# The ordering pass works under its timeline simulation of engines and transfers instead of its simpler estimate: a transformer block on one core

## The chip, the core and the metric

One Trainium2 chip, of which the program uses one core. A core has five engines, each with its own queue of instructions: TensorE (PE, matrix products), VectorE (DVE), ScalarE (ACT), GpSimd (POOL) and SyncE (SP, which here only starts transfers). The metric is the device time of one execution in microseconds (us); of several runs the median is taken.

## The reference, cut to what matters

One block over 1024 tokens of width 1024, with 256 context tokens in front of it:

```python
px = split_proj(modulate(layer_norm(x), ...) @ w_in)            # q, k, v of attention; q, k, v, z of the delta rule; two gates
# differential attention, 8 heads: two softmaxes over 1280 keys, subtracted
p = softmax(q @ k.T); a = p[0] - lam * p[1]; o_da = rms_norm(a @ v)
# gated delta rule, 8 heads, forward and backward in time: a recurrence over chunks
for chunk: v_new = u - w @ state; o = q @ state + qk @ v_new; state = state * g + k.T @ v_new
y = (sigmoid(g1) * (o_da @ w_br_da) + sigmoid(g2) * (o_dn @ w_br_dn)) @ w_o
h = layer_norm(alpha * h + gate * y); h = layer_norm(alpha * h + gate * (relu(u @ w1) ** 2 @ w2))
```

All is fp32. A large product is done as three products of split operands (a high and a low part each).

## The kernel before

The code names operations and tiles; a pass of the library then puts all instructions of the program in one order. It goes through the program with a priority for each instruction and an estimate of when engines and transfers are free, gives each engine the ready instruction of the first priority, and writes the order out. Each engine then runs its own instructions in exactly that order, and waits on semaphores where an operand isn't there. So nothing is chosen at run time: what the pass put behind a waiting instruction on the same engine waits too. The code sets the priorities by `rank`: in the stages below a recurrence or a softmax has class 0, its preparation 1, and the projections that fill the gaps come after them.

The stages, in the order of time:

1. Norms, modulation, projections of the context.
2. The delta rule (`dn_phase`), head by head. For head h: `dn_proj` (a projection of `cvraw`, then seven taps of a convolution: one on ACT and six on DVE for each of two parts, L440, into `kT`, `qT`, `vT`), `dn_prep` (decays, L467 and L470; Gram matrices, L520 and L528; a triangular inverse on DVE, `inverse32`), `dn_double` (small products that complete the inverse, L611 to L633), then `dn_chain`: ten steps in each of two directions, each step L676, a DVE operation (L678), L680, ACT (L683, L686), L688, DVE (L693), and the output (L698, L699, and on DVE L706, L707). At its end the output of the head, `oacc`, is normed (L715 to L719) and transposed on PE (L723). `kT` and `qT` have two buffers each, so the taps of head h + 2 wait until the last step of head h has read them.
3. Attention (`da_all`): 64 tiles of 128 queries, eight for each head. `da_scores` of a tile: score products into `sx` (two maps, 1024 keys each) and `sc` (256 context keys), L877 and L878; maxima on DVE (L887 to L889), exponentials on ACT (L893, L894) into `p`, sums and the difference of the maps on DVE (L897 to L903). `da_values` of a tile, one tile later in the code: ten transposes of `p` into one bank `pat` (L913) in groups of 3, 3, 3 and 1, each group copied out into `aT` by ACT, DVE, ACT and ACT (L914), then ten products with `V` (L916), then `oh` (L917, L918). `p` of map 0 has one buffer, of map 1 two; each `sx` has one.
4. Merge of the branches, norms, and the MLP (L974 to L976, L1370).

The fillers are the projections, three products of 128x512 for each of eight blocks of the width and two halves of the tokens (`gemm_cols`, L164 to L166): 48 for one weight. They need nothing of the recurrence or the softmax that runs beside them. Three weights, 144 products, belong to the next head in the attention stage. In the last attention head the products of `branch_dn` (L974 to L976) take their place.

## Time and profile before

| | |
|---|---|
| median of three runs | 3041.43 us (3039.56 to 3043.84) |
| the profiled execution: its time, its span | 3038.64 us, 3036.9 us |
| PE busy | 93% of the span |
| DVE, ACT, POOL busy | 66%, 44%, 22% |
| granted TensorE clock, mean | 0.958 |

The span runs from the first instruction to the last. An engine's busy share is a mean over stages that are limited in different ways. [...]

### The profile page before, as it was taken

To read this page: it belongs to the slowest core of one execution; us is meant where nothing else is said; L and a number is where in the kernel's file an instruction comes from. 1 tells how busy PE (TensorE), PEld (TensorE's weight loads), DVE (VectorE), ACT (ScalarE), POOL (GpSimd) and SP (SyncE) were. 2 spreads that over 40 slices of the span, in tenths; PEclk is the share of its full clock that TensorE was granted. 3 is DMA by queue.
4 is the path that set the end of the run, shared out by engine and by line. 5 is a ranking of instruction groups with operands and counts; after the bars stand their busy time and mean duration, and the time that the engine had idled before them with its cause. 6 is when DMAs were issued, how large, how long until landed. Compare 5 with 4: busy or idle time off the path is not lost. (4 is left out here: it accounts for less than half of the span.)

```text
span 3036.9 us, 44469 instructions
## 1 busy us (share of the span) xinstructions
PE 2828.2 (93%) x15928; PEld 2273.6 (75%) x15928; DVE 2008.3 (66%) x3675; ACT 1333.1 (44%) x3269; POOL 656.6 (22%) x756
## 2 busy tenths in 40 slices
PE   7998989899898999989999999899999999989998
PEld 4886768677686777868887778677777677768887
DVE  4768497794967767247777778664486776544435
ACT  4655244444443544326655556564465422322210
POOL 1234223532423241021111110101001643100000
PEclk9999799998998999789999999999999999999999
DMA  7631211211212122173433332416564544453321
GB/s 253 190 110 43 52 48 34 67 53 41 70 33 66 34 63 67 37 186 81 105 93 93 91 88 66 91 39 198 158 220 131 164 143 120 137 194 104 104 63 63
DMA packets 340973, 303.09 MB, mean 100 GB/s; under 512 B 87892, under 2 KB 287700, under 8 KB 339728
## 3 DMA queue, kind: packets, MB, share of 16 engines
q1 hardware_dynamic: 318864, 252.14, 28.5%
q10 hardware_dynamic: 18304, 37.41, 4.8%
q0 software_dynamic: 3584, 10.71, 1.0%
q8 instruction: 125, 2.05, 0.3%
q14 instruction: 96, 0.79, 0.1%
HBM read 212.08 MB, written 66.06 MB: 92 GB/s over the span
## 5 line engine op out<-in xcount | busy, mean ns | idle before, releaser
L150 POOL TENSOR_TENSOR wlo<-wraw,whi 128x256 fp32r<-128x256 f32 x312 | 320.7, 1033 | 1219.5 <-ACT whi L149 987.3
L164 PE MATMUL pg<-uh,whi 128*128 128x512 f32 x1152 | 481.7, 418 | 6.6 <-ACT whi L149 3.2
L166 PE MATMUL pg<-uh,wlo 128*128 128x512 f32 x1152 | 481.3, 418 | 6.1 <-POOL wlo L150 5.8
L165 PE MATMUL pg<-ul,whi 128*128 128x512 f32 x1152 | 481.4, 418 | 0.0
L149 ACT CAST whi<-wraw 128x256 fp32r<-128x256 f32 (+1 forms) x568 | 241.0, 430 | 322.9 <-PE pg L165 102.9
L166 PEld LDWEIGHTS pg<-uh,wlo 128*128 128x128 f32 x1152 | 224.6, 195 | 49.9 <-POOL wlo L150 11.1
L164 PEld LDWEIGHTS pg<-uh,whi 128*128 128x128 f32 x1152 | 224.9, 195 | 47.0 <-ACT whi L149 4.8
L165 PEld LDWEIGHTS pg<-ul,whi 128*128 128x128 f32 x1152 | 224.8, 195 | 39.6
L1370 PE MATMUL pa<-B,A 128*128 128x512 f32 x768 | 220.6, 395 | 13.6 <-ACT B L1318 5.0
L1370 PE MATMUL pg<-B,A 128*128 128x512 f32 x768 | 219.5, 393 | 0.0
L150 DVE TENSOR_TENSOR wlo<-wraw,whi 128x256 fp32r<-128x256 f32 (+1 forms) x256 | 136.6, 542 | 120.8 <-ACT whi L149 119.1
L888 DVE TENSOR_REDUCE mp<-sx 128x1 f32<-128x1024 f32 x128 | 155.7, 1218 | 49.8 <-PE sx L878 49.4
L1370 PEld LDWEIGHTS pa<-B,A 128*128 128x128 f32 x768 | 145.9, 190 | 46.9 <-ACT B L1318 5.4
L1370 PEld LDWEIGHTS pg<-B,A 128*128 128x128 f32 x768 | 146.2, 190 | 30.7
L893 ACT ACTIVATE p<-sx,mx 128x1024 f32<-128x1024 f32 x128 | 143.2, 1118 | 53.2 <-DVE mx L889 41.9
L916 PEld LDWEIGHTS pat<-V,aT 128*128 128x128 f32 x1280 | 151.0, 193 | 14.6 <-ACT aT L914 12.1
L916 PE MATMUL pat<-V,aT 128*128 128x128 f32 x1280 | 158.8, 279 | 0.0
L913 PE MATMUL pat<-ident,p 128*128 128x128 f32 x640 | 119.6, 285 | 8.0 <-ACT oh L917 5.0
L1386 DVE TENSOR_TENSOR acc<-pa,acc 128x512 f32<-128x512 f32 x32 | 22.1, 690 | 157.0 <-PE pa L1370 157.0
L1318 ACT CAST A<-araw 128x1024 fp32r<-128x1024 f32 x32 | 33.6, 1052 | 209.7 <-PE pg L1370 171.8
L913 PEld LDWEIGHTS pat<-ident,p 128*128 128x128 f32 x640 | 74.6, 142 | 56.2 <-ACT aT L914 21.3
L877 PE MATMUL sx<-K,Q 128*128 128x512 f32 x256 | 109.5, 428 | 2.9 <-DMA wraw<-in_w_in_dram 2.0
(457 smaller groups left out, 6701.8 us busy)
## 6 DMA issues: line engine op xcount, KB each, us to landing
wraw<-in_w_in_dram SPq DMA_DIRECT2D x288, 128.0 KB
wraw<-in_w_in_dram SPq DMA_DIRECT2D x64, 256.0 KB
uraw<-in_w_mlp_dram SPq DMA_DIRECT2D x32, 512.0 KB
braw<-in_w_mlp_dram SPq DMA_DIRECT2D x32, 512.0 KB
araw<-ff_d SPq DMA_DIRECT2D x32, 512.0 KB
ff_d<-ue SPq DMA_DIRECT2D x52, 256.0 KB
adraw<-in_w_ada_dram SPq DMA_DIRECT2D x32, 320.0 KB
wa<-in_w_ada_dram SPq DMA_DIRECT2D x8, 1024.0 KB
```

What stands on the lines that cost most here:

```text
L149: nc.scalar.copy(out=hi, in_=raw)
L150: self.weng.tensor_tensor(out=lo, in0=raw, in1=hi.bitcast(F32), op=ALU.subtract)
L164: nc.tensor.matmul(o, lhsT=hi, rhs=a, start=k == 0, stop=False)
L165: nc.tensor.matmul(o, lhsT=hi, rhs=b, start=False, stop=False)
L166: nc.tensor.matmul(o, lhsT=lo, rhs=a, start=False, stop=k == KT - 1)
L877: nc.tensor.matmul(ps, lhsT=Q[m][:, qs], rhs=Kh[m][:, ks], start=True, stop=False)
L888: nc.vector.tensor_reduce(out=mp[:, m, 0:1], in_=px[m], axis=AX.X, op=ALU.max)
L893: nc.scalar.activation(out=p[:, CTX:], in_=px[m], func=AF.Exp, bias=mx[:, m:m + 1], accum_out=sp[:, 0, m:m + 1])
L913: nc.tensor.transpose(out=pt[:, c], in_=a[:, (c0 + c) * P:(c0 + c + 1) * P], identity=self.ident)
L916: nc.tensor.matmul(po, lhsT=aT[:, c], rhs=r["v"][:, c], start=c == 0, stop=c == NT - 1)
L1318: nc.scalar.copy(out=z[:, 0], in_=x)
L1370: mm = lambda x, y, **kw: nc.tensor.matmul(ps[c], lhsT=a[:, x, k], rhs=bt[:, y, s], **kw)
```

## The change

One argument of the context that records and orders the program. No operation, tile, buffer or priority changes.

```diff
-    with tile.TileContext(nc) as tc:
+    with tile.TileContext(nc, schedule_with_timeline_sim=True) as tc:
```

The pass still goes by the priorities, but what is ready and free comes from a simulation of the engines' queues and of the transfers. Both programs hold the same instructions on PE, DVE, POOL and SP; ACT has six loads of function tables more (nine instead of three at other lines). The order on every engine differs over the first two thirds of the program; the second product of the MLP (L1370) stands as before.

**Place 1: PE and DVE inside an attention head.** On PE `p` and `pat` belong to a tile's values, `sx` to the scores of a later tile, `pg` is a filler's product. Before, the transposes of one tile (`p_17524`) stand between fillers:

```order
L913 MATMUL pat<-ident,p_17524 128x128 x3
L166 MATMUL pg<-uh,wlo 128x512
L164 MATMUL pg<-uh,whi 128x512
L165 MATMUL pg<-ul,whi 128x512
L166 MATMUL pg<-uh,wlo 128x512
L913 MATMUL pat<-ident,p_17524 128x128 x3
L164 MATMUL pg<-uh,whi 128x512
L165 MATMUL pg<-ul,whi 128x512
L166 MATMUL pg<-uh,wlo 128x512
L913 MATMUL pat<-ident,p_17524 128x128
```

Now, in a tile of the same place (`p_16413`; its copies out of `pat` still come after 3, 3, 3 and 1 transposes):

```order
L913 MATMUL pat<-ident,p_16413 128x128 x9
L877 MATMUL sx_16579<-K_16007,Q_16101 128x512
L878 MATMUL sx_16579<-L_16009,Q_16101 128x512
L877 MATMUL sx_16579<-K_16007,Q_16101 128x512
L878 MATMUL sx_16579<-L_16009,Q_16101 128x512
L913 MATMUL pat<-ident,p_16413 128x128
L916 MATMUL pat<-V,aT 128x128 x10
```

The fillers are gone from between the transposes, and half of the scores of the tile three places on (`sx_16579`) now stand ahead of the last transpose. From the first tile's products with `V` to the last's, every one of the 63 steps held fillers or branch products before (5 to 81); now 53 of the 63 hold none, and the 144 fillers of a head stand in one step, that of its first tile.

On DVE, before, from the difference of the maps of one tile to the two maxima of the next:

```order
L903 SCALAR_TENSOR_TENSOR p_18186<-p_18186,cf,p_18183 128x1280
L887 TENSOR_REDUCE mp<-sc 128x2
L1413 SCALAR_TENSOR_TENSOR adacc<-adraw,s_cols,adacc 128x512
L914 COPY aT<-pat 128x384
L889 TENSOR_REDUCE mx<-mp 128x1
L888 TENSOR_REDUCE mp<-sx_18225 128x1
L889 TENSOR_REDUCE mx<-mp 128x1
```

and now:

```order
L903 SCALAR_TENSOR_TENSOR p_16733<-p_16733,cf,p_16730 128x1280
L888 TENSOR_REDUCE mp<-sx_17081 128x1
L887 TENSOR_REDUCE mp<-sc 128x2
L914 COPY aT<-pat 128x384
L889 TENSOR_REDUCE mx<-mp 128x1 x2
```

The maximum over the second `sx` (L888) moved ahead of the copy (L914) and of the value that the first exponential needs (the first L889).

**Place 2: PE and DVE at the end of a head of the delta rule.** PE before, from the last output product (L699) on; then come 71 more fillers, and behind them L723:

```order
L699 MATMUL po<-wp_6409,pm 128x128
L164 MATMUL pg<-uh,whi 128x512
L165 MATMUL pg<-ul,whi 128x512
L646 MATMUL pt<-ident,vT 128x128 x2
L166 MATMUL pg<-uh,wlo 128x512
L164 MATMUL pg<-uh,whi 128x512
L165 MATMUL pg<-ul,whi 128x512
L166 MATMUL pg<-uh,wlo 128x512
L164 MATMUL pg<-uh,whi 128x512
L653 MATMUL pt<-ident,kT 128x128 x8
L165 MATMUL pg<-ul,whi 128x512
```

and now, from the same head's last step to the transposes of its output:

```order
L680 MATMUL pc_6404<-xs_6406,cm 128x128
L646 MATMUL pt<-ident,vT 128x128 x2
L653 MATMUL pt<-ident,kT 128x128 x4
L699 MATMUL po<-wp_6409,pm 128x128
L653 MATMUL pt<-ident,kT 128x128 x6
L486 MATMUL pt<-ident,kT 128x128 x10
L493 MATMUL pt<-ident,qT 128x128 x4
L723 MATMUL po<-ident,oacc 128x128 x8
```

No filler is left there; all 288 of the head stand earlier, some 20 between one step of the recurrence and the next, and its last six steps hold none. On DVE, now, behind the last step's operation (L678):

```order
L678 SCALAR_TENSOR_TENSOR xs_6406<-pc_6404,necg,vtok 128x128
L440 SCALAR_TENSOR_TENSOR kT<-cvraw,taps,kT 128x772
L440 SCALAR_TENSOR_TENSOR kT<-cvraw,taps,kT 128x516
L440 SCALAR_TENSOR_TENSOR kT<-cvraw,taps,kT 128x772
L440 SCALAR_TENSOR_TENSOR qT<-cvraw,taps,qT 128x508
L440 SCALAR_TENSOR_TENSOR kT<-cvraw,taps,kT 128x516
L440 SCALAR_TENSOR_TENSOR qT<-cvraw,taps,qT 128x516
```

Before, the twelve taps of `kT` stood there one by one between the operations of `inverse32`, the norm of `oacc` (L715 to L719) among them, and the taps of `qT` behind it. Now the inverse stands in the first half of the recurrence, and the 24 taps of `kT` and `qT` stand nearly together ahead of L719.

## Rows read from the trace of the kernel before

**Rows 1.** The page: busy time of each engine, share of the span, instructions.

```profile
PE 2828.2 (93%) x15928; PEld 2273.6 (75%) x15928; DVE 2008.3 (66%) x3675; ACT 1333.1 (44%) x3269; POOL 656.6 (22%) x756
```

**Rows 2.** By stretch: us; PE, PEld, DVE, ACT, POOL busy (instructions); clock; DMA share, GB/s.

```profile
2736.00:2812.00 76.00, 76.00 (x337) 62.93 (x336) 36.37 (x38) 15.62 (x15) 0.00 (x0) 1.00 0.33 104
236.00:1294.70 1058.70, 970.34 (x6528) 783.86 (x6528) 750.86 (x1660) 460.23 (x1301) 344.92 (x407) 0.92 0.20 51
1374.80:2056.40 681.60, 657.23 (x3885) 534.69 (x3883) 497.25 (x849) 407.60 (x1059) 78.03 (x91) 0.99 0.32 82
1471.10:1557.90 86.80, 84.89 (x508) 69.64 (x507) 67.32 (x114) 52.53 (x136) 10.90 (x12) 1.00 0.34 90
```

**Rows 3.** Timeline of ACT in one tile: start, us, engine, operation, idle before.

```profile
1847.87 1.14 ACT L893 ACTIVATE p<-sx,mx 128x1024 f32<-128x1024 f32 x1
...
1853.43 1.12 ACT L893 ACTIVATE p<-sx,mx 128x1024 f32<-128x1024 f32 x1 [1.36 <-DVE mx L889]
...
1854.54 0.47 ACT L914 COPY aT<-pat 128x384 f32<-128x384 f32 x1
...
1855.43 0.27 ACT L914 COPY aT<-pat 128x128 f32<-128x128 f32 x1
1855.59 1.12 ACT L893 ACTIVATE p<-sx,mx 128x1024 f32<-128x1024 f32 x1
```

**Rows 4.** Timeline of DVE in the same tile.

```profile
1851.71 0.69 DVE L887 TENSOR_REDUCE mp<-sc 128x2 f32<-128x512 f32 x1
1852.78 0.56 DVE L914 COPY aT<-pat 128x384 f32<-128x384 f32 x1 [0.38 <-PE pat L913]
1853.26 0.14 DVE L889 TENSOR_REDUCE mx<-mp 128x1 f32<-128x2 f32 x1
1853.32 1.21 DVE L888 TENSOR_REDUCE mp<-sx 128x1 f32<-128x1024 f32 x1
1854.56 0.15 DVE L889 TENSOR_REDUCE mx<-mp 128x1 f32<-128x2 f32 x1
```

**Rows 5.** Timeline of PE at the tile's end and in the next.

```profile
1855.06 0.33 PE L913 MATMUL pat<-ident,p 128*128 128x128 f32 x1
...
1855.93 2.39 PE L916 MATMUL pat<-V,aT 128*128 128x128 f32 x20
...
1861.22 0.50 PE L913 MATMUL pat<-ident,p 128*128 128x128 f32 x3
```

**Rows 6.** Groups by line, DVE, whole span: count, busy us, mean ns, idle before.

```profile
L440 DVE SCALAR_TENSOR_TENSOR kT<-cvraw,taps,kT 128x772 f32<-128x772 f32 x48 | 50.6, 1054 | 0.0
L678 DVE SCALAR_TENSOR_TENSOR xs<-pc,necg,vtok 128x128 f32<-128x128 f32 x144 | 49.9, 348 | 23.9 <-PE pc L676 21.3
...
L440 DVE SCALAR_TENSOR_TENSOR kT<-cvraw,taps,kT 128x516 f32<-128x516 f32 x48 | 39.2, 816 | 5.6 <-ACT kT L438 5.5
...
L440 DVE SCALAR_TENSOR_TENSOR qT<-cvraw,taps,qT 128x516 f32<-128x516 f32 x48 | 37.6, 784 | 0.7
L440 DVE SCALAR_TENSOR_TENSOR qT<-cvraw,taps,qT 128x508 f32<-128x508 f32 x48 | 37.4, 779 | 0.1
...
L719 DVE TENSOR_TENSOR oacc<-oacc,soy 128x1024 f32<-128x1024 f32 x8 | 10.1, 1266 | 0.0
```

**Rows 7.** Waits of PE, 423.4 to 1294.7 us: us in total, times, longest.

```profile
PE po L723 <- DVE oacc L719: 25.8, 7, 11.0
...
PE pt L493 <- ACT qT L442: 5.9, 3, 3.1
```

**Rows 8.** By stretch (columns of rows 2), where PE waits in the attention stage.

```profile
1916.00:1923.00 7.00, 4.45 (x25) 4.15 (x25) 3.71 (x6) 1.39 (x4) 0.00 (x0) 0.74 0.66 53
1923.00:1940.00 17.00, 14.85 (x74) 11.70 (x74) 11.09 (x18) 11.84 (x26) 1.65 (x2) 0.82 0.30 91
```

**Rows 9.** Groups by line, ACT, whole span: loads of function tables.

```profile
L472 ACT ACT_TABLE_LOAD x15 | 19.2, 1283 | 0.3
```

## The prediction

> **What bounds the kernel now.** I read the busy line of the page first, then the busy time by stretch, and then the timeline of one tile. PE is busy for 2828.2 us of a span of 3036.9 us [rows 1], so the whole program has at most some 209 us of idle PE to win back, and far more to lose where PE comes to wait. The stretches say how it is kept busy. In the MLP 337 products of 512 columns take 76.00 us, so such a product costs .2255 us at the full clock [rows 2]. In the delta rule PE is idle for 1058.7 - 970.34 = 88.4 us, at a mean clock of .92; in attention it is idle for 681.6 - 657.23 = 24.4 us, at .99 [rows 2]. One attention head takes 86.8 us, with 84.89 of PE but only 67.32 of DVE and 52.53 of ACT [rows 2]. So PE bounds a head. Its 144 fillers are 144 x .2255 = 32.5 us of it, and what is left, 54.3 us, is 6.8 us for each of eight tiles.
>
> A tile has a second limit, which the fillers hide. From the first exponential of one tile (L893 at 1847.87) to that of the next (1855.59) there are 7.72 us [rows 3]. Between them lie a chain through DVE, ACT and PE: exponentials, sums, the difference of the maps, maxima, transposes, copies, and the next exponentials, each on an engine that goes through its instructions in order. Here PE has other work while this chain runs. Before the change, PE's order and the chain give nearly the same time; what the change does to either decides the result.
>
> **The change, part by part.** No work is added on PE, DVE, POOL or SP. ACT gets six more table loads, each 1.283 us [rows 9], 7.7 us in all. ACT is busy for 44% of the span [rows 1], so I cost them at nothing; if they all lay on the path they would cost 7.7.
>
> *The 53 bare tiles of attention.* PE has no product of its own to fill these steps, so the tile takes as long as the chain. I build the new chain out of the old one.
>
> - It starts at 7.72. In the old one DVE's copy waited .38 us for a transpose that stood behind fillers [rows 4]. Without them this falls away: 7.34.
> - On DVE the second maximum over `sx` (L888, 1.21 us) and the second L889 (.15 us) come ahead of the value for which ACT waits 1.36 us [rows 3, 4]. The first L889 is later by that much: 8.70. (L887, .69 us, stood ahead of it before too [rows 4].)
> - From the end of the second exponential (1853.43 + 1.12 = 1854.55) to the first exponential of the next tile (1855.59) there were 1.04 us [rows 3]. This piece is replaced: 7.66 without it.
> - In its place comes what the order on PE now says: four score products into the `sx` that this exponential frees, 4 x .2255 = .90, and only then the last transpose. From that transpose's start (1855.06 [rows 5]) over its copy (1855.43) to the next exponential (1855.59) there were .53 us [rows 3]. Together 7.66 + .90 + .53 = 9.1 us.
>
> In such a tile PE works for some 5.6 us: 2.39 for the products with `V` [rows 5], about 1.2 for ten transposes (.50 for three [rows 5], less drain) and 2.2 for eight score products of 512 columns and four of 256. This is 62% of 9.1 us. Before the change there are two stretches with a PE about as busy: one with 4.45 of 7.00 us, at a granted clock of .74, and one with 14.85 of 17.00, at .82 [rows 8]. At .74, PE's links in the chain (.90 for the scores, .33 for the last transpose, .50 for a group of three [rows 2, 5]) take 1/.74 = 1.35 times as long: 1.73 x .35 = .6 us. A tile then takes 9.7 us instead of 6.8, and 53 tiles cost 53 x 2.9 = 154 us.
>
> The bounds: if the maximum that came ahead and the scores are hidden, the chain is 7.3 us and costs 53 x .5 = 27 us. [...] I take 154, since the first row of a PE with like work is the one at .74.
>
> [...]
>
> *The ends of the delta-rule heads.* At the end of a head DVE now does 24 taps in a row, in front of the norm of `oacc`: six each of 1.054, .816, .784 and .779 us [rows 6], together 20.6 us, and then L719, 1.27 us [rows 6]: 21.9 us. PE has nothing left in that time but some 30 transposes of 128 columns (L646, L653, L486, L493), at .11 us each (2.39 us for 20 like records [rows 5], with drain) 3.3 us, and of these the ones of `kT` and `qT` wait for the taps too. What is queued behind them on PE is L723 and with it the whole next head, fillers included. So PE waits 21.9 - 3.3 = 18.6 us. In the order of before fillers cover this, and PE waits 25.8 us for `oacc` and 5.9 for `qT` in seven heads [rows 7], 4.5 per head. The change costs 14.1 us per head, and six heads have the taps of a head after the next behind them: 6 x 14.1 = 85 us. The bounds are 0 (the taps run earlier than their place suggests, since DVE has time in the bare steps) and 8 x 21.9 = 175 us. I take 85, because the taps can't start before the head's last step has read the buffers.
>
> *The last six steps of each recurrence.* They hold no filler either. In 48 steps PE waits for DVE's and ACT's hops. A step has two waits for an operation like L678, .348 us [rows 6], and the step of the other direction covers part of that: I take .5 us, 24 us in all. The bounds are 0 (covered) and 48 x 2.4 = 115, where all of a step's seven DVE operations of .348 lie on the path. The 20 fillers that now stand between the earlier hops are 20 x .2255 = 4.5 us, which is more than the hops, so there PE stays busy.
>
> *The rest.* The second product of the MLP keeps its order, and the merge has nearly the same; I cost both at nothing. What hides the waits there is products of 512 columns, and these remain.
>
> The sum: 154 + 85 + 24 = 263 us on the profiled execution's 3038.64 us (1.7 us around the span) gives 3302; the median of the runs is 2.8 us above that execution: 3304, rounded 3305.
>
> **The rivals.** A difference of 0.2%, 6 us, is about what a measurement of this kernel can tell from no change.
>
> - A, the forecast: both stages lose. 3230 to 3430 as its own range. For it: the order on PE fixes what stands where, and PE can't reach past a waiting product to a filler.
> - B: only one of the two stages loses. If the taps find time on DVE ahead of their end (DVE is busy for 750.86 of 1058.7 us in this stage [rows 2], so it has room), the time is 3041 + 154 = 3195. If the attention tile is nearer to its old 7.3 us, it is 3041 + 27 + 109 = 3177. Against it: both are decided by rows of an order that does not adapt.
> [...]
> - D, on the other side: the new order removes the waits of the delta rule. With fillers between all early hops, the 88.4 us of idle PE go [rows 2], the heads' tails cost no more than the 4.5 us of now, and the attention tile stays at 6.8 because its DVE and ACT work runs ahead in the one step that holds 144 fillers. 3041 - 88 = 2953. It decides where PE's wait for `oacc` is below 4.5 us per head and a bare tile below 6.8. Against it: one `sx` of each map and one `p` of map 0 let nothing run far ahead.
> - E: the stages give and take, and it comes out at 3041.
>
> **How the numbers follow.** A has .52, B .19, C .20, D .06, E .03. The predicted time is A's. The range leaves out D, E, a part of B and the far part of C: 3160 to 3510. Faster .06, same .03, slower .91 come from D, E, and A to C.
>
> **What would show it.** In the profile of the changed kernel: bare attention tiles 9 to 10 us apart, with ACT's first exponential waiting for L889 and PE idle for the last transpose; a head of attention at some 107 us (86.8 + 7 x 2.9); a clock of .7 to .85 in attention; PE's wait for `oacc` or for `kT` and `qT` at some 18 us in each of six heads; short waits for L678 and L693 in the last steps; the stretch of the MLP unchanged. I am wrong if PE's busy share in attention stays above 90%, or if the taps are done before the last step of a head ends; and in size if the clock falls to .5, or if a tile's chain passes through a wait that I left out, such as one from an ACT read of `sx` to PE's next scores.

## The result, and the profile after

The changed kernel takes 3399.3 us (median of four runs, 3395.7 to 3401.8) against 3040.5 us of the kernel before: a ratio of 1.1183, with a 95% interval of 1.1153 to 1.1214. The forecast was 3305 with a range of 3160 to 3510, so the direction and the range hold and the size is short by 94 us.

First the busy line of the page after, to be read against [rows 1]: PE has 103 us more busy time with the same instructions, so some of them took longer (the mean granted clock falls from .958 to .916), and its share falls from 93% to 86%.

```profile
PE 2931.3 (86%) x15928; PEld 2384.0 (70%) x15928; DVE 2008.1 (59%) x3675; ACT 1357.4 (40%) x3275; POOL 608.4 (18%) x756
```

Then the busy time by stretch, in the columns of [rows 2]: seven heads of the delta rule, attention, the step of one head that holds the 144 fillers, two bare tiles, and one bare tile that takes far longer than the others.

```profile
425.50:1425.20 999.70, 852.80 (x5657) 699.59 (x5655) 611.97 (x1351) 404.04 (x1101) 248.27 (x332) 0.89 0.18 47
1425.20:2444.20 1019.00, 816.61 (x4148) 661.29 (x4148) 549.58 (x910) 440.27 (x1109) 87.34 (x103) 0.88 0.27 69
1724.50:1773.40 48.90, 44.15 (x208) 36.45 (x209) 26.44 (x43) 15.43 (x35) 8.43 (x11) 0.93 0.33 93
1790.80:1799.80 9.00, 6.60 (x43) 5.22 (x43) 5.62 (x11) 5.08 (x15) 0.00 (x0) 1.00 0.00 1
2313.80:2324.30 10.50, 8.14 (x42) 6.37 (x42) 5.78 (x11) 5.05 (x15) 0.00 (x0) 0.83 0.00 0
1689.30:1704.90 15.60, 9.02 (x42) 6.77 (x42) 8.97 (x13) 7.29 (x17) 0.00 (x0) 0.72 0.57 130
```

The two tiles in the middle do the same work. At a granted clock of 1.00 it takes 9.0 us, where 9.1 was forecast; at .83 it takes 10.5.

The same seven heads of the delta rule in the kernel before:

```profile
423.40:1294.70 871.30, 809.99 (x5557) 656.03 (x5557) 617.04 (x1372) 386.33 (x1099) 282.08 (x331) 0.93 0.20 52
```

So PE stands idle there for 999.7 - 852.8 = 146.9 us, where it was 61.3.

I cut the execution at three events: the first L723 of the first head of the delta rule, that of the last head, and the last tile's products with `V` (L916). This table is made from their start times, and the same cuts serve for the runs below.

| | before | after | difference |
|---|---|---|---|
| up to the first head's L723 | 423.4 | 425.5 | +2 |
| delta rule, seven heads | 871.3 | 999.7 | +128 |
| from there to the last tile of attention | 761.7 | 1019.0 | +257 |
| the rest | 980.5 | 953.3 | -27 |

The rows don't hold equal work. Before, 189 of the 288 branch products (L974 to L976) ran between the tiles of the last head and 99 after them; now all 288 run inside: 99 x .2255 = 22 us moved from the last row to the one above. And the stretch of the delta rule now holds 1872 fillers (L164 to L166), where it held 1768: 104 of them, 23 us, moved there from the stretch below. For equal work the delta rule loses some 105 us and attention some 258.

The waits of PE in seven heads of the delta rule (425.5 to 1425.2 us; total, times, longest), against [rows 7]: the end of a head waits for `kT`, where it waited for `oacc`, and the steps wait for ACT and DVE. (Of the 25.8 us for `oacc` in [rows 7], 11.0 end at 423.4 and so belong to the first head; the seven have 14.8.)

```profile
PE pt L486 <- ACT kT L442: 54.1, 5, 10.9
PE pc L688 <- ACT wp L686: 19.7, 32, 2.0
PE po L723 <- DVE oacc L719: 16.0, 2, 8.4
PE pt L646 <- ACT vtok L648: 15.5, 6, 3.0
...
PE pc L676 <- DVE S L693: 7.5, 18, 1.4
```

The end of the second head, from its last L676 to its first L723, before and then after: PE is busy for 17.56 of 21.00 us, now for 8.07 of 24.70. All 24 taps start in this stretch.

```profile
513.40:534.40 21.00, 17.56 (x85) 13.16 (x83) 20.93 (x49) 12.99 (x43) 7.11 (x6) 1.00 0.19 50
556.40:581.10 24.70, 8.07 (x35) 6.09 (x35) 22.07 (x43) 17.46 (x57) 1.46 (x8) 0.60 0.03 11
```

One bare tile at the full clock, DVE and then ACT, against [rows 3, 4]: L888 stands ahead of the copy and of both L889, ACT waits 1.37 us for them, and from the exponential of the second map in one tile (1790.61) to that in the next (1799.64) there are 9.03 us. The one that waits (1796.88) is that of the first map.

```profile
1793.03 1.55 DVE L903 SCALAR_TENSOR_TENSOR p<-p,cf,p 128x1280 f32<-128x1280 f32 x1
1794.50 1.22 DVE L888 TENSOR_REDUCE mp<-sx 128x1 f32<-128x1024 f32 x1
1795.63 0.68 DVE L887 TENSOR_REDUCE mp<-sc 128x2 f32<-128x512 f32 x1
1796.23 0.55 DVE L914 COPY aT<-pat 128x384 f32<-128x384 f32 x1
1796.70 0.21 DVE L889 TENSOR_REDUCE mx<-mp 128x1 f32<-128x2 f32 x2
```

```profile
1790.61 1.12 ACT L893 ACTIVATE p<-sx,mx 128x1024 f32<-128x1024 f32 x1
...
1796.88 1.11 ACT L893 ACTIVATE p<-sx,mx 128x1024 f32<-128x1024 f32 x1 [1.37 <-DVE mx L889]
...
1799.48 0.27 ACT L914 COPY aT<-pat 128x128 f32<-128x128 f32 x1 [0.57 <-PE pat L913]
1799.64 1.12 ACT L893 ACTIVATE p<-sx,mx 128x1024 f32<-128x1024 f32 x1
```

And ACT in the long tile (1689.3 to 1704.9): the casts of the next head's `K` and `Q` (L826, L843) and its starts of transfers (ACTq) stand between the tile's own operations, and two copies out of `pat` come 1.34 and 2.28 us late behind these starts. This is the shortest of its kind; in the other five, one such copy comes 5.9 to 6.3 us late there.

```profile
1693.70 1.26 ACT L826 CAST K<-rk 128x1280 fp32r<-128x1280 f32 x1 [0.24 <-PE sc L877]
1694.86 1.04 ACT L843 CAST Q<-rq 128x1024 fp32r<-128x1024 f32 x1
...
1700.54 1.23 ACTq L830 DMA_DIRECT2D L<-L  x1
1701.86 0.48 ACT L914 COPY aT<-pat 128x384 f32<-128x384 f32 x1 [1.34 <-issue]
1701.89 1.41 ACTq L847 DMA_DIRECT2D Q<-rsh  x1
1703.34 0.96 ACTq L848 DMA_DIRECT2D Q<-rsh  x1
1704.62 0.27 ACT L914 COPY aT<-pat 128x128 f32<-128x128 f32 x1 [2.28 <-issue]
```

Six of the 53 bare tiles are of this kind, 15.6 to 18.4 us each and 104.1 in all (the fifth tile of six heads). A seventh, of 20.7 us, holds the norm of a head's output (L958, L962), which other heads have in the step of the fillers. The other 46 take 457.7 us, 9.95 us in the mean; of these 9 are between 9.02 and 9.04 us and 13 between 10.4 and 11. Apart from the last tiles, which have no scores to compute, their time follows the granted clock: 8.3 to 9.03 us at 1.00, 10.0 at .86 or .87, 10.5 at .82 to .86, 11.4 to 13.9 at .74 to .78. A whole head of attention takes 117 to 123 us, where some 107 were forecast.

### The profile page after: what moved, and what is told of

The parts are those of the page before. It is cut to its first block, busy times and chain, and to the rows that moved or that the text cites. A ratio compares the mean times of both kernels' runs of the same rounds, so it can differ in the third digit from the quotient of the medians.

```text
span 3397.5 us, 44521 instructions
## 1 busy us (share of the span) xinstructions
PE 2931.3 (86%) x15928; PEld 2384.0 (70%) x15928; DVE 2008.1 (59%) x3675; ACT 1357.4 (40%) x3275; POOL 608.4 (18%) x756
## 5 line engine op out<-in xcount | busy, mean ns | idle before, releaser
L164 PE MATMUL pg<-uh,whi 128*128 128x512 f32 x1152 | 474.2, 412 | 15.2 <-ACT rk L819 8.2
L150 POOL TENSOR_TENSOR wlo<-wraw,whi 128x256 fp32r<-128x256 f32 x312 | 271.4, 875 | 1182.9 <-ACT whi L149 890.7
L166 PE MATMUL pg<-uh,wlo 128*128 128x512 f32 x1152 | 470.9, 409 | 4.6 <-POOL wlo L150 4.4
L165 PE MATMUL pg<-ul,whi 128*128 128x512 f32 x1152 | 471.9, 410 | 0.0
L164 PEld LDWEIGHTS pg<-uh,whi 128*128 128x128 f32 x1152 | 224.3, 195 | 64.5 <-ACT rk L819 8.6
L166 PEld LDWEIGHTS pg<-uh,wlo 128*128 128x128 f32 x1152 | 224.0, 194 | 55.4 <-POOL wlo L150 8.8
L888 DVE TENSOR_REDUCE mp<-sx 128x1 f32<-128x1024 f32 x128 | 156.4, 1222 | 159.6 <-PE sx L878 158.9
L913 PE MATMUL pat<-ident,p 128*128 128x128 f32 x640 | 126.9, 298 | 120.3 <-ACT aT L914 66.1
L916 PEld LDWEIGHTS pat<-V,aT 128*128 128x128 f32 x1280 | 190.1, 237 | 48.9 <-ACT aT L914 48.2
L1370 PE MATMUL pa<-B,A 128*128 128x512 f32 x768 | 219.5, 392 | 5.1 <-ACT A L1318 2.6
L916 PE MATMUL pat<-V,aT 128*128 128x128 f32 x1280 | 201.2, 326 | 24.8 <-ACT aT L914 24.8
L1370 PE MATMUL pg<-B,A 128*128 128x512 f32 x768 | 218.8, 391 | 0.0
L913 PEld LDWEIGHTS pat<-ident,p 128*128 128x128 f32 x640 | 77.7, 148 | 160.7 <-ACT aT L914 83.1
L1370 PEld LDWEIGHTS pa<-B,A 128*128 128x128 f32 x768 | 144.6, 188 | 37.1 <-ACT A L1318 3.0
L1370 PEld LDWEIGHTS pg<-B,A 128*128 128x128 f32 x768 | 144.8, 189 | 29.9
L877 PE MATMUL sx<-K,Q 128*128 128x512 f32 x256 | 121.5, 474 | 42.2 <-ACT p L893 41.2
L914 ACT COPY aT<-pat 128x384 f32<-128x384 f32 (+1 forms) x192 | 78.0, 407 | 160.5 <-PE pat L913 121.6
L693 DVE SCALAR_TENSOR_TENSOR S<-S,edec,pc 128x128 f32<-128x128 f32 x128 | 44.0, 344 | 123.8 <-PE pc L688 123.0
```

Source lines behind the costliest of these rows:

```text
L150: self.weng.tensor_tensor(out=lo, in0=raw, in1=hi.bitcast(F32), op=ALU.subtract)
L164: nc.tensor.matmul(o, lhsT=hi, rhs=a, start=k == 0, stop=False)
L165: nc.tensor.matmul(o, lhsT=hi, rhs=b, start=False, stop=False)
L166: nc.tensor.matmul(o, lhsT=lo, rhs=a, start=False, stop=k == KT - 1)
L888: nc.vector.tensor_reduce(out=mp[:, m, 0:1], in_=px[m], axis=AX.X, op=ALU.max)
L913: nc.tensor.transpose(out=pt[:, c], in_=a[:, (c0 + c) * P:(c0 + c + 1) * P], identity=self.ident)
```

## Experiments

The theory at the start was the forecast: a bare tile costs its chain, and a head of the delta rule costs the taps that stand in front of its norm. Each edit below adds an issue order between two instructions of one engine (`behind(later, earlier)`: no wait, no other work), unless said otherwise. Line numbers in rows of these runs are those of the edited kernels, up to 23 higher than in the text. Each of these kernels but the last two ran once, and the kernel before, run beside them, took 3023 to 3052 us, so I compare stages more than totals.

**Taps behind the norm.** The first DVE tap of each half of `kT` and `qT` is put behind L719 of the head two before.

```diff
+                    if nm != "v" and j == 0 and h >= 2:
+                        behind(self.tc, tap, self.normed)
```

> The changed kernel, with the 24 taps of kT and qT of a head of the delta rule ordered on DVE behind the norm of oacc (L719) of the head two before. My theory (the taps in front of the norm hold up PE at the end of six heads): the 10.9 us waits of PE for kT and the waits for oacc go, a head of the delta rule takes 153 - 15 = 138 us, and the program 6 x 15 = 85 us less than 3399: 3314, in a range of 3290 to 3340. Rival (the delta rule's loss lies in the bare steps of the recurrence and in fillers that moved from the end of a head into it, so the taps only delay the next preparation instead): 3380 to 3400.

It measured 3418.2 us. Seven heads of the delta rule take 1022.2 us instead of 999.7, of which 10 only say that the first head, before the stretch, ended sooner (415.5 instead of 425.5 us); the last ends 12 us later. The waits for `kT` at the end of a head are gone, but others stand there (L729 and L725 are L723 and L719, L652 is L646, L682 to L694 are the steps):

```profile
PE po L729 <- DVE oacc L725: 54.5, 7, 9.4
PE pg L168 <- ACT sz L461: 29.3, 7, 5.2
PE pc L686 <- DVE xs L684: 19.0, 17, 4.7
PE pc L682 <- DVE S L699: 17.9, 26, 2.9
PE pt L652 <- ACT vtok L654: 15.5, 6, 3.0
PE po L617 <- DVE sz L731: 15.3, 6, 2.6
```

So my theory in its first form falls: the place of the taps ahead of the norm is not what costs. The taps can't be done before the head's last step; put behind the norm they hold up the steps and the preparation of the next head.

**Fillers at the end of a head.** The two gate projections of each head, 96 products, are put on PE behind the last first product (L676) of its recurrence; the taps stay.

```diff
-                    nc.tensor.matmul(pc[:, 0], lhsT=self.ck(kT, c), rhs=S0, start=True, stop=True)
+                    self.step = nc.tensor.matmul(pc[:, 0], lhsT=self.ck(kT, c), rhs=S0, start=True, stop=True)
...
+                if self.gate_at and k == 0:
+                    behind(self.tc, m, self.gate_at)
...
                 if c == "f":
+                    self.gate_at = self.step
                     self.fill(1)
+                    self.gate_at = None
```

> The changed kernel, with the two gate projections of each head of the delta rule (96 products, 21.6 us) ordered on PE behind the first product of the last step of the recurrence; the taps stay where the change put them. The run with the taps behind the norm left the head at 154 us, so the place of the taps is not the cause. My theory, mended (the taps cost because no filler is left for the end of the head, and cost as much in any place without one): PE's waits of 10.9 us for kT go under cover, a head goes from 153 to some 135 us, and the time is 3399 - 6 x 18 = 3290, in a range of 3260 to 3330. Rival (DVE's serial work of a head, or the longer recurrence of 105 us instead of 55, sets the 153 us): the recurrence gets shorter by 21 us, the end longer by as much, and the time stays within 3380 to 3410.

It measured 3293.5 us. Seven heads take 902.8 us instead of 999.7, the first five 133 to 134 us each instead of 149 to 156, and no wait for `kT` or `qT` is left:

```profile
PE pc L694 <- ACT wp L692: 21.7, 40, 3.1
PE pc L682 <- DVE S L699: 9.1, 21, 1.8
PE po L729 <- DVE oacc L725: 8.4, 1, 8.4
PE pc L686 <- DVE xs L684: 7.5, 15, 0.7
```

The whole stretch, and then the end of the second head, to be read against the rows above:

```profile
417.20:1320.00 902.80, 839.48 (x5697) 687.12 (x5695) 607.23 (x1351) 399.83 (x1105) 273.92 (x337) 0.95 0.21 53
521.80:551.10 29.30, 29.30 (x142) 23.98 (x142) 24.66 (x44) 19.03 (x59) 12.81 (x16) 1.00 0.25 74
```

The recurrence, from its first L680 to its last L699, shrank from some 104 us to 80, as the rival said, but from there to the next L723 there are 18 to 20 us in both, so the end didn't grow. From the last L676 on, PE is busy for all of the 29.3 us, 113 fillers among them. What cost was that PE had used up its fillers when the taps came. And nothing of the loss is left: PE is idle for 63.3 us, as in the kernel before (61.3), and the 31.5 us above that kernel's 871.3 are 140 more fillers (1908 instead of 1768, 31.6 us), which ran outside this stretch before.

**The first maximum first.** L888 of the second `sx` is put behind the first L889.

```diff
-            nc.vector.tensor_reduce(out=mp[:, m, 0:1], in_=px[m], axis=AX.X, op=ALU.max)
-            nc.vector.tensor_reduce(out=mx[:, m:m + 1], in_=mp[:, m], axis=AX.X, op=ALU.max, negate=True)
+            mi = nc.vector.tensor_reduce(out=mp[:, m, 0:1], in_=px[m], axis=AX.X, op=ALU.max)
+            if m:
+                behind(self.tc, mi, first)
+            first = nc.vector.tensor_reduce(out=mx[:, m:m + 1], in_=mp[:, m], axis=AX.X, op=ALU.max, negate=True)
```

> The changed kernel, with the maximum over the second sx (L888) ordered on DVE behind the first L889. My theory (the chain of a bare tile is a sum of its links, of which this is one): the first exponential comes 1.4 us earlier, but the copy that DVE makes out of pat then stands behind the maximum, so that a bare tile at clock 1.00 goes from 9.03 to some 8.3 us, and 53 tiles save 30 to 60 us: 3340 to 3370. Rival (PE at its lower clock is what limits a bare tile): tiles stay at 9 to 10.5 us and the time at 3399 within 10.

It measured 3352.4 us; attention takes 971.0 us instead of 1019.0, 48 less. The total is as expected, the way to it is not: a plain tile takes 8.88 us, not 8.3, only .15 us less than 9.03. But 36 bare tiles are under 9.05 us, where the changed kernel has 15. A stretch of two of them:

```profile
1879.20:1897.00 17.80, 13.26 (x84) 10.66 (x84) 11.66 (x20) 10.46 (x29) 0.00 (x0) 1.00 0.00 1
```

The plain tiles of 10 to 10.5 us are nearly gone. Plain tiles give 28 of the 48 us: 46 x .15 = 7 by the shorter chain, and 21 with tiles that now stand at the full clock. The rest lies in the tiles with rotary work (12) and in the steps with fillers (13), less 4 lost ahead of the first tile, while the mean granted clock of the execution is .933 instead of .916. Why it stays up with this order, no run here tells.

**Idle time filled.** Four transposes of the identity, which nobody reads, behind each of the first three groups of L913 in every tile, and the next group behind them.

```diff
+EXTRA = 4
...
+            for x in range(EXTRA if c0 < 9 else 0):
+                extra = nc.tensor.transpose(out=po, in_=self.ident, identity=self.ident)
+                behind(self.tc, extra, m)
```

> The changed kernel, with twelve more transposes of the identity in each of 64 tiles on PE (four behind each of the first three groups of L913, into a part of pat that is overwritten later), which no one reads: 12 x .11 = 1.3 us of PE per tile, 85 us in all. My theory (a bare tile takes 9.03 us when the clock is granted in full, and up to 10.5 where it falls because PE waits): the extra work fills waits, the clock in the bare stretches rises from .83 to above .95, the bare tiles without rotary work go from a mean of 9.95 to 9.1 to 9.5, and the time falls by 10 to 45 us, to 3355 to 3390. Rival (the clock costs nothing in a bare tile, as the chain's links on PE are short): the time rises by 20 to 85 us, to 3420 to 3485.

It measured 3397.2 us; attention takes 1010.2 us instead of 1019.0. That is no clear difference: in the first two runs, which don't touch it, it took 1028.1 and 1020.4. But the tiles have changed. Three in a row:

```profile
1789.20:1817.20 28.00, 23.04 (x163) 19.60 (x163) 16.73 (x30) 15.74 (x43) 0.00 (x0) 1.00 0.00 1
```

They take 9.31 us each, all at the full clock, and so do 29 bare tiles of the stage. 768 useless transposes cost nothing on balance. The clock part of the theory is borne out (a tile of 10.5 becomes one of 9.31), but the extra work lengthens the undisturbed chain by .28 us and the second tile of each head from 8.3 to 10.1, so the total gives back the gain; 10 to 45 us were expected, and 2 came. The rival, which had the time rise by 20 to 85, is out.

**Transfers started by SP.** The nine starts at L829 to L831 and L846 to L848 move from `nc.scalar` to `nc.sync`.

```diff
-                nc.scalar.dma_start(out=b[hi_], in_=a[hi_])
+                nc.sync.dma_start(out=b[hi_], in_=a[hi_])
```

> The changed kernel, with the nine transfers that copy halves of K, L and Q of the next attention head started by SP instead of ACT. In the profile after, one bare tile of each head takes 16 to 20 us: the rotary work of the next head (L827, L845 on DVE, L826, L843 on ACT) stands in its chain, and ACT stands 1.34 and 2.28 us idle at two copies out of pat while its queue starts transfers. My theory (both add to the chain, since nothing covers it): the long tiles lose some 3.5 us each, seven of them 25 us: 3375, in a range of 3360 to 3390. Rival (DVE and ACT work of the rotary alone makes the long tile, and ACT's transfers lie beside it): 3399 within 8.

It measured 3381.1 us; attention takes 1005.3 us, 14 less. The six tiles with rotary work fall from 15.6 to 18.4 us to 12.6 to 13.3, and some tiles behind them get longer, one to 19.5. What ACT waited for ahead of its copies (L914) in attention of the changed kernel tells why:

```profile
  PE pat L913: 121.6, 118
  DMA L<-L: 26.5, 5
  issue: 9.9, 3
```

With the starts on SP there is one such row, `PE pat L913` (144.6 us, 127 times). So a part of the long tile was ACT's queue behind its own starts and behind the landings that they wait for. The 3 us or so that are left above a plain tile I put down to the work of L826, L827, L843 and L845; no run took it away.

**Fillers paced by tile.** The projections of the next attention head are named in eight pieces, and a piece of 18 products is put behind the products with `V` of the tile before it.

```diff
+PACE = 6
...
+                m = nc.tensor.matmul(ps, lhsT=hi, rhs=a, start=k == 0, stop=False)
+                if self.gate_at:
+                    behind(self.tc, m, self.gate_at)
...
-            nc.tensor.matmul(po, lhsT=aT[:, c], rhs=r["v"][:, c], start=c == 0, stop=c == NT - 1)
+            self.gate_at = nc.tensor.matmul(po, lhsT=aT[:, c], rhs=r["v"][:, c], start=c == 0, stop=c == NT - 1)
...
+                for _ in range(PACE if t < NX - 1 else 1000):
+                    next(steps, None)
```

> The changed kernel, with the projections of the next attention head named in eight pieces of 18 products, each piece ordered on PE behind the last product with V of the tile before; the last head's branch products stay as they are. My theory (bare tiles cost because the chain of a tile has nothing to hide behind): 42 of the 53 bare tiles get fillers, seven heads of attention go from some 120 to 90 us, the granted clock there to above .97, and the time is 3399 - 6 x 30 = 3220, in a range of 3190 to 3260. Rival (the order of DVE's maxima and of PE's score products is the cause, not the missing fillers): the chain stays at 9 to 10 us per tile and the time within 3370 to 3410.

It measured 3455.8 us, slower than the change by 56, where I had expected 180 less. The pass put the fillers of a tile in blocks ahead of the scores and of the first transposes, and most tiles take 14 to 16 us. PE, with the first of six fillers in a row and the scores that follow them, and DVE, which waits for these (L183 is L164, L900 and L901 are L877 and L878, L910 is L887):

```profile
1795.18 0.48 PE L183 MATMUL pg<-uh,whi 128*128 128x512 f32 x1
...
1796.65 0.39 PE L900 MATMUL sx<-K,Q 128*128 128x512 f32 x1
...
1797.47 0.29 PE L901 MATMUL sc<-L,Q 128*128 128x256 f32 x1
```

```profile
1797.80 0.69 DVE L910 TENSOR_REDUCE mp<-sc 128x2 f32<-128x512 f32 x1 [2.69 <-PE sc L901]
```

So it isn't the number of fillers in a tile that hides its chain. Here a filler in front of a product on which the chain waits is one more link of it.

**Fillers between the transposes.** The same pieces, but six products between each group of three transposes and the next.

```diff
+                if c == 0 and self.gate_at:
+                    behind(self.tc, m, self.last)
...
+            for _ in range(2 if c0 < 9 else 0):
+                self.gate_at = m
+                if next(self.steps, 1):
+                    self.gate_at = None
```

> The changed kernel, with the projections of the next attention head again in pieces, but now six products ordered between one group of three transposes (L913) and the next, three times in each tile, where the run 'paced' left the 18 products of a tile in blocks ahead of the first transposes and got tiles of 15.5 us. My theory, mended by that run (a filler hides a link only where it stands behind an instruction on which the chain goes on elsewhere; ahead of it, it is one more link): the waits of .57, .73 and .75 us in a bare tile are filled, 9.0 us grow to 11 to 11.5 with 4.06 us of fillers, a head of attention takes 90 us instead of 120, and the time is 3399 - 7 x 29 = 3195, in a range of 3160 to 3240. Rival (with the new order of maxima and scores, fillers add to a tile wherever they stand): tiles of 13 to 15 us and a time of 3380 to 3460.

It measured 3309.7 us; attention takes 930.5 us, 88 less than the change. Inside a head it does what was expected: its steps take 9.9 to 12.9 us, 11.2 in the mean, and a steady tile with 18 fillers 10.45 us, at the full clock and with PE nearly always busy. The tile at the change of heads takes 25 to 31 us, which was not expected, and so the time lies far above the 3160 to 3240 of the theory. Its stretch, and then that of two tiles behind it:

```profile
1676.00:1706.80 30.80, 16.19 (x68) 12.38 (x68) 13.84 (x29) 7.90 (x20) 0.87 (x2) 0.67 0.26 78
1707.00:1727.00 20.00, 19.10 (x116) 16.16 (x115) 16.07 (x25) 11.03 (x29) 1.87 (x3) 1.00 0.23 54
```

PE waits there for the exponential that frees `sx` (5.3 us), for the norm of the head's output (L958 on DVE, 4.0 us) and for its copies (L964 on ACT, behind a transfer, 4.1 us); the order of before covered most of these.

**The old order, made bare.** The kernel before, with the 144 fillers put behind the products with `V` of a head's first tile and ahead of the transposes of its second.

```diff
+                if self.gate_at and k == 0:
+                    behind(self.tc, m, self.gate_at)
...
+                if t == 1 and c0 == c == 0:
+                    behind(self.tc, m, self.last)
```

> The kernel before, with its own estimate, but with the 144 fillers of the next attention head ordered on PE between the products with V of a head's first tile and the transposes of its second: 42 tiles become bare as in the change, while DVE keeps its old order (L888 behind the copy and the first L889) and PE the scores in smaller pieces. My theory (a bare tile costs its chain; the old chain is 7.72 - .38 = 7.3 us, the new one 9.0): 42 x .5 = 21 us for the chain, some 20 for the clock and up to 40 for rotary work that nothing covers: 3041 + 40 to 90 = 3080 to 3130. Rival 1 (bareness alone makes the loss of attention): 3041 + 170 to 220 = 3210 to 3260. Rival 2 (the DVE order alone makes it): 3041 within 15.

It measured 3248.3 us beside 3045.7 for the kernel before: attention takes 968.4 us instead of 761.7, 207 more. The total is the first rival's, and mine was a third of it. Steady tiles, two in a row, are close to my chain, at 7.84 us instead of 7.3; but the tile at the change of heads, with the norm, takes 18.9 us (the second row), the step with the fillers 45 to 46 (39.3 would be 32.5 and one covered tile), and the tile behind it 9 to 13:

```profile
1573.60:1589.30 15.70, 13.21 (x86) 10.12 (x85) 11.65 (x20) 10.27 (x29) 0.00 (x0) 1.00 0.08 22
1589.30:1608.20 18.90, 10.47 (x51) 7.14 (x50) 9.72 (x24) 6.56 (x17) 0.00 (x0) 0.72 0.10 35
```

So most of what bareness costs is not the steady tile. It is the work at the change of heads (norm, copies, rotary work, transfers) that nothing covers. Bareness in the old order makes some 210 of the 258 us of attention (15 products moved behind the stage here, 3 us); the 48 that are missing are as many as the first maximum gave back, but no run has both.

**All four edits.** Fillers between transposes, fillers at the end of a head, the first maximum first, and SP's starts, in one kernel.

> The changed kernel with four edits at once: six fillers between groups of transposes, 96 fillers at the end of each head of the delta rule, L888 behind the first L889, and the nine transfers started by SP. If the named places are the whole loss, their sum is 200 + 105 + up to 20 us, since max and transfers are largely covered by fillers now: 3080, in a range of 3040 to 3130. If something that no run has touched (table loads, other orders) has a share, it stays above 3150.

It measured 3209.4 us, a ratio to the kernel before of 1.0563 (1.0516 to 1.0610). The delta rule takes 901.9 us, attention 938.4. The 3080 expected are missed by far: it stays above 3150, the mark for a loss that these edits don't reach. The delta rule holds the same 140 fillers more as above, so it loses nothing; what is left lies in attention. There 81 of the 257 us are back, no more than with the fillers alone (88): with fillers between the links, the other two edits have little left to win. The change of heads still takes 28 to 32 us. Less its 18 fillers, that is some 26 us, against some 11 in most heads of the kernel before (26.5 us with 68 fillers): some 80 us over six heads.

**The kernel before, with SP's starts.** The edit of the transfers alone, in the order pass of before.

> The kernel before, with the nine transfers of K, L and Q started by SP instead of ACT. My theory (ACT's transfers cost only where a tile is bare): in the old order fillers cover them, and the time is that of the kernel before within 8 us. Rival (ACT's queue starting transfers costs in either order): 20 us faster.

It measured 3023.2 us against 3035.7 for the kernel before run beside it, a ratio of .9955 (.9933 to .9977): 13 us or .45% faster, small but clear, and between the two expectations, neither of which holds. This is the one version that beats both kernels. In its profiled execution attention takes 740.1 us instead of 761.7, but 17 us of that are 74 branch products that now run after it (1227 products of fillers and branch in the stage instead of 1301). Since the moved starts shift instructions in the order like this, that ACT's queue is the reason is not shown.

## Why the prediction came out as it did

The sum against the cuts, in us (forecast, measured):

| | forecast | measured |
|---|---|---|
| 46 plain bare tiles, against 6.8 each | 133 | 145 |
| 6 bare tiles with the next head's rotary work | 17 | 63 |
| 1 bare tile with a head's norm | 3 | 14 |
| 5 steps with 144 fillers, against 39.3 each (32.5 and one covered tile) | 0 | 32 |
| the rest of attention, with products moved in (22) and out (-23) | 0 | 3 |
| delta rule: PE idle at the heads' ends, last L676 to first L723 | 85 | 79 |
| delta rule: PE idle in the steps before | 24 | 32 |
| delta rule: PE idle ahead of the steps | 0 | -25 |
| delta rule: 104 fillers moved in | 0 | 23 |
| delta rule: the other products, taking longer | 0 | 19 |
| start, and all after attention (-22 moved out) | 0 | -25 |
| sum | 262 | 360 |

**The chain of a bare tile** was right. 9.03 us stand at the full clock, against 9.1 from seven rows, with ACT's wait of 1.37 us for L889 where it was looked for. (What the prediction calls a tile's first exponential, at 1847.87 and 1855.59, is that of its second map; the one at 1853.43 is the first. The links are the same.) Its two pieces are near as well: 6.54 and 2.55 us in the sum, 6.27 and 2.76 in the trace, so two small errors cancel.

**The clock** was right in kind and wrong in price, and that the mean came near, 9.95 instead of 9.7, is in part luck. The sum put every tile at .74 and let 1.73 us of PE's work in the chain grow, .6 us. By that a clock of .83 adds .35 us; the tile shown is 1.5 us longer. Many tiles at the full clock made up for it. Neither the full clock nor a low one holds throughout: like tiles stand at both 1.00 (9.0 us) and .83 (10.5 us). In the traces of both kernels the clock reads either 1.00 or .50, and a figure between them is a mean: in the tile of 10.5 us it is 1.00 from 2317.0 to 2322.0 us, where a score product of 512 columns (L878) is on record with .40 us, and .50 from 2322.7 to 2323.9, where one is with .63. (PE's work in a tile, 2.39 + 1.2 + 2.2, is 5.8 us and not the 5.6 of the prediction.) That more work on PE went with a higher clock is seen in one run, the one with idle time filled: .932 instead of .916 in the mean, and bare tiles of 9.31 us at 1.00.

**The step that failed** is "53 tiles cost 53 x 2.9": it took all bare tiles for alike. In six of them the next head's rotary work and its transfers stand in the chain, in one a head's norm, and the seven take 17.8 us in the mean. The fillers of before covered more than the steady chain, and I priced the removal of that cover for the chain alone. The steps that now hold a head's 144 fillers were taken for filled ones, 39.3 us, and take 43.0 to 49.3. The run with the old order made bare says it most clearly: 7.84 us for steady tiles and 18.9 for the one at the change of heads. In the tiles with rotary work ACT's queue has a part: its waits ahead of its copies, 26.5 us for the landing of `L` and 9.9 at issue, are gone when SP makes the starts.

**The ends of the delta-rule heads** were right in place and near in price, and wrong in one part of the cause. PE is idle there for 101.2 us in seven heads, where it was 22.4, and for 16.6 at each end with taps, where 18.6 were forecast; the steps give 32 us instead of 24. The wait of before was read too high (4.5 us per head holds the 11.0 of the first; without it, 3.0), and only five of the seven ends that the cuts hold have taps, so the 85 has some luck in it. Left out were the heads' beginnings, which got 25 us better, and products that take longer. But "in front of the norm" doesn't matter: behind it the taps cost 12 us more. What matters is that no filler is left, as the run with 96 of them at the end shows: there PE's idle time is that of the kernel before.

**Rival B** is out, since both stages lose. **C**, with .20 of the chances and a part of the range, took a low clock in all bare stretches; no run shows one, and the 53 bare tiles stand at .67 to 1.00 in the mean, 14 of them at 1.00. **D** and **E** failed at their own points: a bare tile is above 6.8 us, and a head's end above 4.5. The six table loads are 7.7 us of ACT at most; no run took them away.

**What stays open:** some 170 us between all four edits and the kernel before, nearly all in attention. Some 80 of them lie at the change of heads, whose cost is read from steps and waits and was not taken away by a run. And why the clock falls in one bare tile and not in a like one.

## What to carry to other kernels

Before an order is changed, list what each filler covers, in the steady loop and at its seams (the next head's preparation, norms, transfers); a bare loop costs its chain, but bare seams cost more (here 9.03 us a tile at the full clock, and 15.6 to 20.7 at the seams). A filler hides a wait only where it stands behind the product on which the chain goes on; ahead of one, it is a link: 18 of them made tiles of 10.45 us in the one place and of 14 to 16 in the other. Count the work that a stretch holds before comparing its time: here 140 fillers more looked like a loss of 31 us. When a wait is found where it was forecast, move its supposed cause as well: here the taps cost as much in another place.

## What the runs showed of the hardware

Useless work was free on balance where PE waited: 768 more transposes left the total at 3397 us, since tiles of 10.5 us at .83 became 9.31 us at the full clock while those of 9.03 became 9.31 too. Starts of transfers held up ACT's queue: the three shown in the long tile last .96 to 1.41 us each (the shortest there .47; what of that is waiting is not shown), ACT's copies came up to 6.3 us late behind them, and with nine such starts per head on SP the six long tiles fell from 15.6 to 18.4 us to 12.6 to 13.3, while some tiles behind them got longer.
